# Decode scores of a hybrid decoder step: multiply-and-sum on VectorE, or products on VectorE and sums on ScalarE

## The chip, the cores and the metric

The kernel runs on one core of a Trainium2 chip. The metric is the device time of one execution in microseconds (us). TensorE (PE) multiplies matrices, with PEld its weight loads; VectorE (DVE), ScalarE (ACT) and GpSimd (POOL) work on tiles; SyncE (SP) issues transfers, and so does GpSimd. Each engine takes its instructions in the order in which the program wrote them and waits at each for what it needs.

## The reference

One layer of a decoder: a prompt of 512 rows and 32 sample rows (8 sequences of 4 new tokens), 2048 channels. One input projection feeds four branches of 512 channels (a gated MLP "A", a convolution "B", the forgetting attention "C", FoX, and an attention into 256 memory tokens "M"). Each branch is gated, projected back to 2048 channels, weighted by a sigmoid and added; an output projection and a layer norm follow. All is fp32.

The change is in the attention of the sample rows. In branch C each of the 8 sequences has 1024 cached keys and values, in 8 pages of 128 rows that a page table scatters over a pool; in branch M it has 256 memory keys, 2 pages of 128:

```python
logits = einsum('bqhd,bkhd->bhqk', q, k_all) * HD ** -0.5    # 4 heads of 128 channels, 4 queries
logits = logits + (cq[..., None] - ck[:, :, None, :])        # FoX only
out = einsum('bhqk,bkhd->bqhd', softmax(logits), v_all)
```

So there are (8 x 8 + 8 x 2) = 80 pages, and for each of them 4 queries x 4 heads = 16 columns of scores (128 keys by one), 1280 in all.

## The kernel before, in words

**Pieces.** The matrix work is a list of 677 pieces, one after the other. A piece loads a weight block of 128 x 512 numbers (L257, SP), splits it into a high and a low part (L237 a Copy on ScalarE, L238 a subtraction on VectorE, tile `whl`, four buffers, three pieces ahead; loads run four further) and does 24 matmuls of 272 columns (L268, `mm_k`). By number: 0 to 15 are the projection Q_C, 16 the forget gate, 17 to 32 K_C, 33 to 48 V_C, 49 to 64 Q_M, 65 to 96 the memory projections (every second of these carries side work), 97 to 112 V_A, 113 to 128 U_A, 129 to 144 G_A, 145 to 224 the gates of branch A (`add_gates`: eight times eight pieces with sigmoids at the end, then two with a product), 225 to 240 G_M, 241 to 320 the gates of M, 321 to 336 A_B, 337 to 352 B_B, 353 to 368 G_C, 369 to 448 the gates of C, and so on. Eight pieces share one accumulation, two pieces in the branch projections; then it is evacuated from four PSUM banks: the first half of the columns right behind the last piece's matmuls (`std_mm`, `evac_col`), the second half at the start of the next.

**Side work.** Everything else is written as Python generators, whose `yield`s are the places where the program goes on with the matmuls. In `std_mm`, ahead of its own matmuls, each piece runs a few steps of two chains (`side.step`; a `yield 1` ends the chain's turn for this piece, so such a generator gets one step a piece), then some steps of the score generator (`side.vector(rate(p.i))`). The order of the instructions in every engine's queue is the order in which this program ran.

**Scores.** `v_scores` is started by the second step of `t_qtok("qc")`, so that piece 19 is the first with `side.vector`. It goes through the 80 pages: three sequences of C, all eight of M, the other five of C. A page of keys is gathered into one of the two buffers of `kr` (by GpSimd from the page table, L775, or by SP for the memory, L584), the four queries of a sequence are spread over the partitions into `qb` (one buffer, SP, L590). For each of 16 (query, head), L604 multiplies 128 columns of `kr` and `qb` and adds them up into one column of the score tile `L` (`Lm` for M), then yields.

**Decode.** After the last page of C, `t_decode("qc")` is added to chain 0: forget biases (`t_bias`, 5 steps), transposes, softmax and the transposed weights (steps 6 to 12), then 16 rounds (two groups of four sequences, eight pages each), two steps a round; a round is eight records of matmuls (L756) with four gathered pages of values, `vr`, and the loads run two rounds ahead (`load_v(i + nv)`). `final` then writes the result over the queries. It is wanted in `ev_gate` of G_C, first called behind the matmuls of piece 360; what is not done then is run to its end at once, without matmuls in between:

```python
if br not in B:
    side.finish(*[tasks[t] for t in wait])      # ("ac", "dqc") for brC
```

For branch M the same holds behind piece 232 (`dqm`).

**Slots.** Large tiles share 18 slots; one that is given a slot waits until its last user is done. Eight hold the input rows (`xh`, `xl`) throughout. `qb` holds one while the scores run.

Of the kernel before, what the change touches and what calls it, by code (L numbers as in the profile page):

```python
# [10 lines left out]
AF = mybir.ActivationFunctionType  # L11
ALU = mybir.AluOpType
# [7 lines left out]
NPG = 8  # L20
# [69 lines left out]
def hybrid_step(ctx: ExitStack, tc: tile.TileContext, I, O):  # L90
    nc = tc.nc
    V, S, G, T, SP = nc.vector, nc.scalar, nc.gpsimd, nc.tensor, nc.sync
# [9 lines left out]
    def nm(p):  # L102
        cnt[0] += 1
        return f"{p}{cnt[0]}"

    def slot(shape, dt=F32, n="slot"):
        return big.tile(shape, dt, tag="slot", bufs=18, name=nm(n))

    def kt_t(shape, dt=F32, n="kt"):
        return big.tile(shape, dt, tag="kt", bufs=3, name=nm(n))  # L110

    def s2(shape, dt=F32, n="s2"):
        return big.tile(shape, dt, tag="s2", bufs=5, name=nm(n))
# [10 lines left out]
    def ct(shape, dt=F32, n="c"):  # L124
        return const.tile(shape, dt, name=nm(n))
# [13 lines left out]
    side = Side()  # L139
# [132 lines left out]
    def std_mm(p):  # L272
        mv = p.mov()
        n = p.steps
        if marks["dw"] <= p.i < marks["pw"] and pieces[p.i - 1].last:
            n = (n[0], 0)
        side.step(n)
        side.vector(rate(p.i))
        for c in range(2):
            for k in range(2):  # L280
                mm_k(p, mv, c, k)
            side.flush()
        if p.last:
            p.later = evac_col(p, 0)
# [50 lines left out]
    tasks = {}  # L335
# [218 lines left out]
    S_ = {}  # L554

    def t_qtok(k):
        sm = sample(B[k])
        yield
        b = ps()
        tok_major(B[k], 4, b, sm)  # L560
        yield
        t = s2([32, 512], n="qt")
        V.tensor_copy(out=t, in_=b[0:32])
        SP.dma_start(out=qscr[k], in_=t)
        if k == "qc":
            side.vec = v_scores()
        yield

    def v_scores():
        batches = [("qc", b, NPG) for b in range(3)] + [("qm", b, 2) for b in range(8)] + \  # L570
                  [("qc", b, NPG) for b in range(3, 8)]
        S_["qc"] = kt_t([128, 1056], n="L")
        kr = kt_t([128, 2, 512], n="kr")
        qb = slot([128, 4, 512], n="qb")
        pages = [(k, b, pg, i) for i, (k, b, n) in enumerate(batches) for pg in range(n)]
        done = {"qc": 0, "qm": 0}

        def load_page(n):
            if n < len(pages):
                k, b, pg, _ = pages[n]  # L580
                if k == "qc":
                    gpage(kr[:, n % 2], ck, b, pg)
                else:
                    SP.dma_start(out=kr[:, n % 2], in_=cmk[b, pg * 128:(pg + 1) * 128].rearrange("p h d -> p (h d)"))  # L584

        def load_q(i, t):
            if i < len(batches):
                k, b, _ = batches[i]
                r = b * 4 + t
                SP.dma_start(out=qb[:, t], in_=qscr[k][r:r + 1].rearrange("o c -> (o c)").partition_broadcast(128))  # L590

        load_page(0)
        for t in range(4):
            load_q(0, t)
        for _ in range(24):
            yield
        for n, (k, b, pg, i) in enumerate(pages):
            if k == "qm" and k not in S_:
                S_[k] = s2([128, 256], n="Lm")
            for t in range(4):  # L600
                for h in range(4):
                    o = pg * 128 + h * 32 + b * 4 + t
                    junk = S_["junk"] if "junk" in S_ else S_.setdefault("junk", ct([128, 128], n="junk"))
                    V.tensor_tensor_reduce(out=junk, in0=kr[:, n % 2, h * 128:(h + 1) * 128],  # L604
                                           in1=qb[:, t, h * 128:(h + 1) * 128], op0=ALU.mult, op1=ALU.add, scale=1.0,
                                           scalar=0.0, accum_out=S_[k][:, o:o + 1])
                    yield
                if t == 0:
                    load_page(n + 1)
                if t == 0 and pg == 0 and i:  # L610
                    load_q(i, 3)
                if t and pg == batches[i][2] - 1:
                    load_q(i + 1, t - 1)
            if pg == batches[i][2] - 1:
                done[k] += 1
                if done[k] == 8:
                    tasks["d" + k] = side.add(t_decode(k), 0)

    def t_new():

# [152 lines left out]
    def gpage(dst, src, b, pg):  # L773
        j = b * NPG + pg
        G.indirect_dma_start(out=dst, out_offset=None, in_=src,  # L775
                             in_offset=bass.IndirectOffsetOnAxis(ap=idx[:, j:j + 1], axis=0))
# [31 lines left out]
    def m_mm(p):  # L808
        side.step(p.steps if p.wi == 0 else (0, 0))
        side.vector(rate(p.i) if p.wi == 0 else 0)  # L810
        m = mem["T"][:, p.kt // 2 % 2]
        if p.kt == 0:
            for j in range(2):
                mem["a", p.wi, j] = accb()
        for j in range(2):
            for mp, wp in ((0, 0), (0, 1), (1, 0)):
                T.matmul(out=mem["a", p.wi, j], lhsT=m[:, mp, (2 * (p.kt % 2) + j) * 128:(2 * (p.kt % 2) + j + 1) * 128],  # L817
                         rhs=p.w[:, wp], start=p.kt == 0 and mp == 0 and wp == 0, stop=p.kt == 15 and mp == 1)
        side.flush()
# [515 lines left out]
    marks = {}  # L1335
# [27 lines left out]
            pieces.append(p)  # L1363

    def rate(i):
        return 4 if i < marks["gates"] else 5

    at = {
        marks["conv"]: lambda: side.add(t_cconv(), 1),
# [11 lines left out]
    with tc.manual_schedule():  # L1381
        n = len(pieces)
# [113 lines left out]
```

## Time and profile before

Three runs: 1960.68, 1962.4 and 1965.9 us, median 1962.4.

| | |
|---|---|
| the profiled execution's own time | 1961.29 us |
| its span | 1959.6 us |
| TensorE busy, share, matmuls | 1930.0 us, 98%, 14687 |
| weight loads | 1859.4 us, 95% |
| VectorE | 1221.3 us, 62% |
| ScalarE | 621.2 us, 32% |
| GpSimd | 233.4 us, 12% |

Busy time is the union of the instructions on an engine. TensorE's matmuls are pipelined, so its busy share is not its share of the peak. The score loop's first instruction starts at 108.1 us, its last at 1010.5 us.

### The profile page before, as it was taken

To read this page: it belongs to the slowest core of one execution; us is meant where nothing else is said; L and a number is where in the kernel's file an instruction comes from. 1 tells how busy PE (TensorE), PEld (TensorE's weight loads), DVE (VectorE), ACT (ScalarE), POOL (GpSimd) and SP (SyncE) were. 2 spreads that over 40 slices of the span, in tenths; PEclk is the share of its full clock that TensorE was granted. 3 is DMA by queue.
4 is the path that set the end of the run, shared out by engine and by line. 5 is a ranking of instruction groups with operands and counts; after the bars stand their busy time and mean duration, and the time that the engine had idled before them with its cause. 6 is when DMAs were issued, how large, how long until landed. Compare 5 with 4: busy or idle time off the path is not lost.

```text
span 1959.6 us, 38230 instructions
## 1 busy us (share of the span) xinstructions
PE 1930.0 (98%) x14687; PEld 1859.4 (95%) x14687; DVE 1221.3 (62%) x4107; ACT 621.2 (32%) x1164; POOL 233.4 (12%) x265
## 2 busy tenths in 40 slices
PE   8999999999999999999999999999999999999997
PEld 7999989999999899999999889999999999999985
DVE  4265797877777778877763238767645323256687
ACT  3222353444223222222222223222243222244442
POOL 0000100010000001121225430110110101010000
PEclk9999999999999999999999999999999999999999
DMA  5444465324555544444437663333323333346664
GB/s 167 112 121 113 141 194 153 94 80 135 165 175 176 168 138 121 132 135 117 137 97 209 191 181 87 87 90 89 87 76 90 89 87 88 90 138 219 202 213 161
DMA packets 211601, 261.85 MB, mean 134 GB/s; under 512 B 18251, under 2 KB 171355, under 8 KB 210617
## 3 DMA queue, kind: packets, MB, share of 16 engines
q1 hardware_dynamic: 200297, 224.55, 40.0%
q0 software_dynamic: 10544, 33.80, 5.6%
q8 instruction: 115, 1.88, 0.4%
q10 hardware_dynamic: 576, 1.05, 0.1%
q14 instruction: 69, 0.57, 0.1%
HBM read 250.85 MB, written 8.49 MB: 132 GB/s over the span
## 4 chain that ended last, share of the span: by engine, by line
PE 81%; DVE 3%; DMA 2%; issue 1%; ACT 1%; SPq 0%; POOL 0%; DVEq 0%; ACTq 0%; POOLq 0%
PE acc L268 72%; PE acc L1272 3%; PE acc L817 2%; DMA raw<-in_w_out_dram 1%; PE ps L756 1%; DVE whl L238 1%; DMA qb<-qqm 0%; DVE junk L604 0%; DMA vr<-in_cache_mem_v_dram 0%; PE ps L849 0%; PE ps L870 0%; PE ps L507 0%; PE ps L533 0%; DVE cvt L1082 0%; PE ps L1212 0%
## 5 line engine op out<-in xcount | busy, mean ns | idle before, releaser
L268 PE MATMUL acc<-xh,whl 128*128 128x272 f32 x7168 | 1233.9, 290 | 4.1 <-DVE sg L901 2.5
L268 PEld LDWEIGHTS acc<-xh,whl 128*128 128x128 f32 x7168 | 1021.4, 189 | 23.0 <-ACT whl L237 7.5
L237 ACT ACTIVATE whl<-raw 128x512 fp32r<-128x512 f32 x664 | 418.3, 632 | 1129.1 <-PE acc L268 974.5
L238 DVE TENSOR_TENSOR whl<-raw,whl 128x512 fp32r<-128x512 f32 x664 | 464.4, 703 | 461.7 <-ACT whl L237 459.0
L268 PE MATMUL acc<-xl,whl 128*128 128x272 f32 x3584 | 740.1, 288 | 0.0
L268 PEld LDWEIGHTS acc<-xl,whl 128*128 128x128 f32 x3584 | 564.1, 189 | 0.0
L604 DVE CUSTOM_DVE_ANT_0 junk<-kr,qb 128x128 f32<-128x128 f32 x1280 | 379.4, 296 | 49.8 <-DMA qb<-qqm 8.9
L268 PE MATMUL acc<-bh,whl 128*128 128x272 f32 x1024 | 176.1, 289 | 1.3 <-ACT gs L918 1.3
L930 POOL TENSOR_TENSOR h<-h,gs 128x272 f32<-128x272 f32 x96 | 79.1, 851 | 608.1 <-DVE gs L929 608.0
L268 PEld LDWEIGHTS acc<-bh,whl 128*128 128x128 f32 x1024 | 146.2, 188 | 2.0 <-ACT gs L918 1.5
L775 POOL DMA_INDIRECT kr<-in_cache_k_dram,idx x64 | 65.7, 1027 | 683.4 <-DVE L L604 496.9
L268 PE MATMUL acc<-hh,whl 128*128 128x288 f32 x512 | 107.0, 298 | 0.0
L268 PE MATMUL acc<-bl,whl 128*128 128x272 f32 x512 | 105.6, 288 | 0.0
L1098 DVE SCALAR_TENSOR_TENSOR yb<-hb,wdwc,yb 128x512 f32<-128x512 f32 x120 | 93.4, 778 | 2.1
L604 DVE DVE_READ_ACCUMULATOR2_ANT L<- 128x1 f32 x1024 | 83.5, 82 | 0.0
L268 PEld LDWEIGHTS acc<-hh,whl 128*128 128x128 f32 x512 | 83.4, 188 | 0.1
L268 PEld LDWEIGHTS acc<-bl,whl 128*128 128x128 f32 x512 | 80.5, 189 | 0.0
L268 PE MATMUL acc<-hl,whl 128*128 128x288 f32 x256 | 75.5, 295 | 0.0
L775 POOL DMA_INDIRECT vr<-in_cache_v_dram,idx x64 | 65.5, 1023 | 57.1 <-PE ps L756 40.5
L1272 PE MATMUL acc<-whl,hh 128*128 128x512 f32 x216 | 68.0, 395 | 0.3 <-DVE whl L238 0.2
L918 ACT ACTIVATE gs<-acc 128x272 f32<-128x272 f32 x128 | 43.8, 395 | 47.0 <-PE acc L268 46.3
L1272 PEld LDWEIGHTS acc<-whl,hh 128*128 128x128 f32 x216 | 40.4, 188 | 10.0 <-DVE whl L238 0.8
(326 smaller groups left out, 1093.8 us busy)
## 6 DMA issues: line engine op xcount, KB each, us to landing
raw<-in_w_in_dram SPq DMA_DIRECT2D x446, 256.0 KB, 2.8
raw<-in_w_out_dram SPq DMA_DIRECT2D x128, 256.0 KB, 3.5
raw<-in_w_branch_dram SPq DMA_DIRECT2D x64, 256.0 KB, 2.7
qb<-qqc SPq DMA_DIRECT2D x32, 256.0 KB, 4.3
qb<-qqm SPq DMA_DIRECT2D x32, 256.0 KB, 4.0
raw<-in_w_mem_k_dram SPq DMA_DIRECT2D x16, 256.0 KB, 2.7
raw<-in_w_mem_v_dram SPq DMA_DIRECT2D x16, 256.0 KB, 3.6
kr<-in_cache_mem_k_dram SPq DMA_DIRECT2D x16, 256.0 KB, 3.2
```

Source lines behind the costliest of these rows:

```text
L237: S.activation(out=hi, in_=src, func=AF.Copy)
L238: side.later(lambda: V.tensor_tensor(out=lo, in0=src, in1=hi.bitcast(F32), op=ALU.subtract))
L268: T.matmul(out=p.st[c][i][:, 0:hi - lo], lhsT=p.w[:, wp, k, c * 128:(c + 1) * 128], rhs=mv[mp][:, p.k0 + k, lo:hi], start=p.first and k == ...
L604: V.tensor_tensor_reduce(out=junk, in0=kr[:, n % 2, h * 128:(h + 1) * 128], in1=qb[:, t, h * 128:(h + 1) * 128], op0=ALU.mult, op1=ALU.add ...
L756: T.matmul(out=ob[32 * j:32 * j + 32, :], lhsT=PT[:, pg, 4 * g + j, :], rhs=vr[:, j, :], start=pg == 0, stop=pg == npg - 1 and not fox)
L775: G.indirect_dma_start(out=dst, out_offset=None, in_=src, in_offset=bass.IndirectOffsetOnAxis(ap=idx[:, j:j + 1], axis=0))
L817: T.matmul(out=mem["a", p.wi, j], lhsT=m[:, mp, (2 * (p.kt % 2) + j) * 128:(2 * (p.kt % 2) + j + 1) * 128], rhs=p.w[:, wp], start=p.kt == ...
L918: S.activation(out=sgs[0][:, c, hf, :], in_=a, func=AF.Sigmoid)
L930: G.tensor_tensor(out=hd, in0=hd, in1=s, op=ALU.add)
L1098: V.scalar_tensor_tensor(out=yv, in0=hv, scalar=wdw[:, j, c:c + 1], in1=yv, op0=ALU.mult, op1=ALU.add)
L1272: T.matmul(out=oacc[p.nb, j], lhsT=hhl[p.kt // 4][mp][:, p.kt % 4, o:o + 128], rhs=p.w[:, wp], start=p.kt == 0 and mp == 0 and wp == 0, st ...
```

## The change

The score loop works on half a page of queries at a time. One VectorE product forms the 1024 columns of two queries (the page's keys are read twice, by a repeated operand) in one of the two halves of a new tile `prod`, which holds a slot while the scores run; eight ScalarE Copies with an accumulated output then sum 128 columns each. The sums of one half come behind the product of the next (`behind`). Every product and every sum is a step. The loads of the next sequence's queries are issued two and two behind the products of the last page, and the score generator runs five steps a piece throughout.

```diff
@@ -594,27 +594,38 @@
+        prod = slot([128, 2, 2, 512], n="prod")
+        junk = ct([128, 128], n="junk")
+
+        def sums(k, b, pg, half):
+
+            for t in range(2):
+                for h in range(4):
+                    o = pg * 128 + h * 32 + b * 4 + 2 * half + t
+                    S.activation(out=junk, in_=prod[:, half, t, h * 128:(h + 1) * 128], func=AF.Copy,
+                                 accum_out=S_[k][:, o:o + 1])
+                    yield
+            if half and pg == dict(qc=NPG, qm=2)[k] - 1:
+                done[k] += 1
+                if done[k] == 8:
+                    tasks["d" + k] = side.add(t_decode(k), 0)
+
+        behind = iter(())
         for n, (k, b, pg, i) in enumerate(pages):
             if k == "qm" and k not in S_:
                 S_[k] = s2([128, 256], n="Lm")
-            for t in range(4):
-                for h in range(4):
-                    o = pg * 128 + h * 32 + b * 4 + t
-                    junk = S_["junk"] if "junk" in S_ else S_.setdefault("junk", ct([128, 128], n="junk"))
-                    V.tensor_tensor_reduce(out=junk, in0=kr[:, n % 2, h * 128:(h + 1) * 128],
-                                           in1=qb[:, t, h * 128:(h + 1) * 128], op0=ALU.mult, op1=ALU.add, scale=1.0,
-                                           scalar=0.0, accum_out=S_[k][:, o:o + 1])
-                    yield
-                if t == 0:
+            for half in range(2):
+                V.tensor_tensor(out=prod[:, half], in0=kr[:, n % 2].unsqueeze(1).to_broadcast([128, 2, 512]),
+                                in1=qb[:, 2 * half:2 * half + 2], op=ALU.mult)
+                yield
+                if half == 0:
                     load_page(n + 1)
-                if t == 0 and pg == 0 and i:
-                    load_q(i, 3)
-                if t and pg == batches[i][2] - 1:
-                    load_q(i + 1, t - 1)
-            if pg == batches[i][2] - 1:
-                done[k] += 1
-                if done[k] == 8:
-                    tasks["d" + k] = side.add(t_decode(k), 0)
+                if pg == batches[i][2] - 1:
+                    for t in range(2):
+                        load_q(i + 1, 2 * half + t)
+                yield from behind
+                behind = sums(k, b, pg, half)
+        yield from behind
 
@@ -1363,7 +1374,7 @@
     def rate(i):
-        return 4 if i < marks["gates"] else 5
+        return 5
```

## Rows read from the trace of the kernel before

**Rows 1.** The page's span and busy times: engine, busy us, share, instructions.
```profile
span 1959.6 us, 38230 instructions
...
PE 1930.0 (98%) x14687; PEld 1859.4 (95%) x14687; DVE 1221.3 (62%) x4107; ACT 621.2 (32%) x1164; POOL 233.4 (12%) x265
```

**Rows 2.** Waits of TensorE: waiter, releaser, us in total, times, longest.
```profile
PE ps L993 <- DVE cA L989: 3.0, 1, 3.0
...
PE acc L268 <- DVE h L927: 1.1, 1, 1.1
...
PE acc L268 <- ACT ua L941: 0.5, 1, 0.5
```

**Rows 3.** Windows: stretch, us, busy time (instructions) of PE, PEld, DVE, ACT, POOL, clock, DMA.
```profile
625.00:1012.00 387.00, 385.72 (x3073) 381.45 (x3072) 296.17 (x1468) 103.04 (x192) 60.45 (x70) 1.00 0.47 135
```

**Rows 4.** Windows, around the wait of L993; the granted clock is third from last.
```profile
378.00:381.20 3.20, 0.24 (x2) 0.02 (x1) 3.15 (x8) 0.63 (x1) 0.00 (x0) 0.96 0.30 79
381.20:384.40 3.20, 3.17 (x15) 3.14 (x16) 2.99 (x20) 0.00 (x0) 0.00 (x0) 0.50 0.14 20
```

**Rows 5.** Groups by line and form, L604: busy us, mean ns, idle before, releasers.
```profile
L604 DVE CUSTOM_DVE_ANT_0 junk<-kr,qb 128x128 f32<-128x128 f32 x1280 | 379.4, 296 | 49.8 <-DMA qb<-qqm 8.9 <-DMA qb<-qqc 5.6 <-DVE Lm L604 0.8
...
L604 DVE DVE_READ_ACCUMULATOR2_ANT L<- 128x1 f32 x1024 | 83.5, 82 | 0.0
...
L604 DVE DVE_READ_ACCUMULATOR2_ANT Lm<- 128x1 f32 x256 | 20.9, 82 | 0.0
```

**Rows 6.** Groups by line and form, nearest operations: products, copies, Exp, a table load.
```profile
L237 ACT ACTIVATE whl<-raw 128x512 fp32r<-128x512 f32 x664 | 418.3, 632 | 1129.1 <-PE acc L268 974.5 <-issue 68.3 <-PE acc L1272 20.2
...
L1082 DVE TENSOR_TENSOR cvt<-hs,wdwc 128x992 f32<-128x992 f32 x4 | 8.0, 1991 | 0.0
...
L234 DVE TENSOR_TENSOR hl<-h,hh 128x1024 fp32r<-128x1024 f32 x4 | 4.9, 1218 | 0.0
...
L766 DVE COPY Oall<-ps 128x512 f32<-128x512 f32 x4 | 2.8, 690 | 10.4 <-PE ps L760 7.8 <-PE ps L756 2.7
...
L485 ACT ACTIVATE P<-P,nmx 128x512 f32<-128x512 f32 x4 | 2.9, 724 | 6.2 <-DVE nmx L483 6.2
...
L485 ACT ACTIVATE P<-P,nmx 128x128 f32<-128x128 f32 x4 | 1.6, 402 | 1.5 <-DVE nmx L483 1.5
...
L941 ACT ACT_TABLE_LOAD x2 | 2.6, 1283 | 0.0
```

**Rows 7.** Timeline of ACT, an Exp with accumulated output: start, us, instruction.
```profile
388.39 0.51 ACT L485 ACTIVATE P<-P,nmx 128x256 f32<-128x256 f32 x1 [0.38 <-DVE nmx L483]
388.81 0.19 ACT L485 ACTIVATION_READ_ACCUMULATOR P<-P,nmx 128x1 f32 x1
388.90 0.50 ACT L485 ACTIVATE P<-P,nmx 128x256 f32<-128x256 f32 x1
```

**Rows 8.** Timeline of PE around the end of piece 360.
```profile
1165.74 1.06 PE L756 MATMUL ps<-vr,PTs 128*32 128x512 f32 x8
1166.74 1.06 PE L760 MATMUL ps<-rows,PnT 32*32 32x512 f32 x8
...
1170.83 0.60 PE L746 MATMUL ps<-ident,Oall 128*128 128x128 f32 x4
1172.82 0.74 PE L268 MATMUL acc<-xh,whl 128*128 128x272 f32 x2 [1.39 <-DVE sg L901]
```

**Rows 9.** The chain that ended last, 1054 to 1062 us: start, us, what.
```profile
1054.37 1.00 PE ps L756 x8
...
1061.57 1.00 PE ps L756 x8
```

**Rows 10.** Timeline of POOL: the first two gathers behind round 0.
```profile
1055.74 0.95 POOL L775 DMA_INDIRECT vr<-in_cache_v_dram,idx  x1 [10.30 <-PE ps L756]
1056.99 0.95 POOL L775 DMA_INDIRECT vr<-in_cache_v_dram,idx  x1 [0.30 <-issue]
```

**Rows 11.** One line, L775 (all gathers): from issue to landing.
```profile
DMA to landing us min/median/max: 3.2/3.8/5.8
```

## The prediction

> **What bounds the kernel now.** I read the page's busy times first [rows 1]: TensorE is busy for 1930 of the span's 1959.6 us. Then its waits [rows 2]: of what is left, the score stage (108 to 1011 us) has three that the change can touch, 3.0 us for L989's copy, 1.1 us for L927, 0.5 us for a GELU (L941). Then the stretches [rows 3]: where the score loop runs longest undisturbed, 625 to 1012 us, TensorE is busy 385.7 of 387 us beside a VectorE at 77% and a ScalarE at 27%. So TensorE sets the pace, and taking work off VectorE is worth only what those waits cost. One of them costs twice: after the 3 us of idleness before L993 the granted clock is 0.50 (the lower level, 1.2 GHz) from 381.2 to 384.4 us [rows 4], so that one piece of 3.0 us took about 1.5 us more. The most to be won is 3.0 + 1.5 + 1.1 = 5.6 us.
>
> **What the scores cost now and will cost.** L604's 1280 instructions are 379.4 us and the reads of the accumulator 83.5 and 20.9 [rows 5]: 484 us of VectorE. The new product has 1024 columns, two SBUF operands, fp32; nearest is L234's 128x1024, 1.22 us, and the far bound L1082's product with a strided broadcast operand, 1.99 us for 992 columns [rows 6]. Here the broadcast operand repeats a whole row of 512, columns adjacent, so I take 1.22: 160 x 1.22 = 195 us, 289 us less for VectorE (165 us less at 1.99).
>
> ScalarE gets 1280 ACTIVATEs of 128 columns, each with a read of its accumulator. The trace has the pair only as Exp over 256 columns: 0.51 us from one start to the next, the read adding 0.09 of it beyond the ACTIVATE's end [rows 7]. A Copy of 512 columns from SBUF takes 632 ns, and Exp 402 ns for 128 columns and 724 for 512, so 0.84 ns a column [rows 6]: a Copy of 128 is some 632 - 384 x 0.84 = 309 ns, less 0.09 of overlap with what follows, plus 0.09 for the read, 0.31 us a sum. Bounds: 0.22 (the read free) to 0.50 (309 + 190 ns, nothing overlapped). I take 0.31, nearest to rows 7: 1280 x 0.31 = 397 us on top of ScalarE's 621 [rows 1]. Five steps a piece, 40 sums in 45 of them, are 4.44 x 0.31 = 1.4 us; with the weight split (about 0.54 of its 0.63 us not overlapped) 1.9 us of a piece's 3.0. L237 waited 974 us for TensorE in all [rows 6], so ScalarE has the room on average.
>
> Per score the two engines together will be busy about 0.46 us (0.31 + 195/1280), against 0.38 (484/1280) before. The Trainium skill, "ScalarE: Activation LUTs", Rules for kernel authors, speaks against such a move: additions and multiplications belong on VectorE, not ScalarE; it calls VectorE up to about three times faster per element in bf16. By that rule, which the two figures bear out in sign (in fp32 and by less), the work is dearer where it goes, and ScalarE could become the bound: the first rival below.
>
> **What is lost on ScalarE.** Its queue is in order, and a piece's sums stand ahead of its own evacuation. In plain pieces an evacuation after 0.54 + 5 x 0.31 us is ready at 2.8 us, before TensorE wants the bank at 3.0. Where a table load of 1.28 us stands ahead of it as well (six evacuations: L941, L938 and L900, two each, one of these rows in [rows 6]) the cover is thinner: L941 already made TensorE wait 0.5 [rows 2], so 1.5 us more are bare there; a second such place gives perhaps 1.0, a third 0.4; the others have room. 2.9 us; bounds 0 and 6 x 1.55 = 9.3. The product waits for the last sum of two halves before, which is issued just ahead of it; that holds up VectorE's weight subtraction, queued behind, by up to 2 us, but it is wanted only three pieces (9 us) later. The query loads move up: all four are issued 17 steps (some 10 us) ahead of their use, and the waits for them in front of the score instructions [rows 5], behind which L927's 1.1 us came about, should go. On SP's queue they hold up weight loads by at most one product; these run four pieces ahead.
>
> **When the scores end.** Count the calls of the score generator from piece 19 on. Before: pieces 19 to 64, 16 memory pieces, pieces 97 to 144, 110 in all at 4 calls = 440, then 5 a piece. It ends in call 24 + 1280 + 1 = 1305, and (1305 - 440)/5 = 173 pieces after 144: piece 317. After: 550 calls by piece 144, and 24 + 160 + 1280 + 1 = 1465 in all, since each product is a step too: (1465 - 550)/5 = 183, piece 327. The memory scores end at piece 184 instead of 189; both are far ahead of 232, where they are wanted. The FoX decode starts one piece later, one step a piece: round i of its 16 weighted sums (L756) is its step 13 + 2i. Before, round 15 fell on piece 360 exactly, the piece whose evacuation wants the decode finished (`side.finish` in `ev_gate`, brC). The trace shows this [rows 8]: round 15 and L760, one piece of matmuls, the last transposes, then the first gate with a wait of 1.39 us. **After, piece 360 carries round 10, and rounds 11 to 15 run in one burst behind it.**
>
> **What the burst costs.** Spaced two pieces apart (7.2 us) [rows 9] the rounds hid their gathers; in the burst nothing does. A round needs four gathers, 1.25 us apart on GpSimd [rows 10], the last landing 3.8 us after its issue [rows 11]: 7.6 us from the first. A gather into a slot starts about 0.4 us after the round that frees it (round 0 ends at 1055.4, the next gather starts at 1055.74). At piece 360 fifteen of 18 slots hold other tiles, the convolution's `yb` takes one more there, two are left for pages. With t = 0 at round 10: it ends at 1.0, piece 360 at 4.1, round 11 at 5.1, round 12 at 6.1 (both loaded). Round 13's gathers start when 11 has freed its slot, 5.5, ready 13.1. Round 14's: GpSimd is free at 10.5, ready 18.1. Round 15's: slot free at 14.5, GpSimd at 15.5, ready 23.1. Then 1.0 + 1.0 (L760), a copy of 512 columns 0.7 (L766, [rows 6]), transposes 0.6, copy and gate 0.9 (less than the 1.39 of [rows 8], which held other work too): the next piece at 27.3. TensorE's own work in this is 1 + 3 + 5 + 1 + 0.6 = 10.6, idle 16.7; before 1.39. That is +15.3. By [rows 4] an idle time of 3 us puts the clock to 0.50: the end of the burst (2.6 us of matmuls) at half clock costs +2.5. Together +17.8. Bounds: with a third slot free, round 13's gathers start at round 10's end, which saves 4 us, and with the clock kept up 2.5 more: +11; with every landing at the longest of [rows 11], 5.8, and half clock into the next piece: +22.
>
> **Sum.** -5.6 + 2.9 + 17.8 = +15.1 us on the profiled execution's 1961.3 us (1.1 us below the median of 1962.4): 1976.4 us.
>
> **Rivals.** (1) ScalarE becomes the bound. With 0.50 us a sum, the last piece of a sigmoid pair puts 0.54 + 2.5 + 0.7 (two sigmoids of 272 columns, by the same slope) = 3.7 us ahead of TensorE's next bank at 3.0; 18 such pairs (eight in each of two gate stages, two of G_M) x 0.7 = 13 us: 1989. For it: Exp's read lasts 0.19 us. Against it: only 0.09 of that is left bare [rows 7].
> (2) The other side: the burst is covered and the kernel is faster. GpSimd's queue does not follow the pieces, only its slots; with four or more slots free for pages at piece 360 the gathers of rounds 13 to 15 would be under way before TensorE comes to them, and the finish would cost no more than the 1.4 us of before. Then 1961.3 - 5.6 + 0 to 2.9 = 1956 to 1959. Against it: the gather of [rows 10] sat idle for 10.3 us until round 0 freed its slot.
> (3) Half a burst: the scores run out earlier than counted or TensorE finds more pages there, and one or two rounds are bare: some 7 us, 1966. For it: the count rests on every yield.
>
> **Chances.** Forecast 0.66 (own range 1967 to 1986; 0.04 of it within 0.3%). Rival 1 0.10, slower. Rival 2 0.16, half of it faster by over 0.3% (5.9 us, about what a measurement of this kernel tells from no change), half within. Rival 3 0.08, within. Slower 0.62 + 0.10 = 0.72, within 0.04 + 0.08 + 0.08 = 0.20, faster 0.08. The range, 1962 to 1990, leaves out rival 2 and the ends of the forecast's own spread.
>
> **What would show it.** Right: after the scores, in front of brC's first gate, L756 with waits for `vr` gathers of 4 to 7 us and granted clock 0.50 there; sums on ScalarE 0.3 us apart; no wait before L993; VectorE some 290 us less busy. Wrong: L756 at that place without waits (rival 2), or TensorE waiting for ScalarE's evacuations all through the gate stages (rival 1); the prediction fails if the finish in front of brC costs under 10 us.

## The result and the profile after

The changed kernel takes 2013.22 us (median of 4 runs, 2011.22 to 2015.14), the kernel before 1962.72 beside it: a ratio of 1.0258 [1.0246, 1.0271]. That is 50 us more, where 15 were forecast and 28 were the upper end of the range. The sign was right, the size was not.

The page of the changed kernel, span and busy time of each engine (as [rows 1]):

```profile
span 2009.6 us, 38549 instructions
...
PE 1952.5 (97%) x14687; PEld 1865.9 (93%) x14687; DVE 1046.1 (52%) x1707; ACT 1093.1 (54%) x3724; POOL 248.3 (12%) x265
```

TensorE has its 14687 matmuls as before, and yet 22 us more of busy time. That isn't more work. Some 3.4 us of it are two more stretches at half clock (an estimate: in each, 3.4 us of busy time do the work of 1.7; they are shown below). Of the rest, much is waiting that is shown as work: matmuls' ends are modelled, and where a group of them trickles, waiting for its operands, part of the wait counts as busy. The Trainium skill, "Perfetto Trace Analysis", Tensor Engine Instruction, says that TensorE's end times are computed from the instruction's size, not observed. The trace agrees: the burst below is some 8 us of work and shows 15.76 us of busy time. So the lost time is better read from the start of the same piece in both traces than from waits. Each piece has a fixed number of matmuls, so counting them finds the piece. Time gained (-) or lost by each kernel against the one before, in us, worked out in this way from one profiled execution of each (the columns behind the changed kernel's are experiments of the next section):

```
                               before's   changed  two    sums   both   changed  two tiles+last
pieces (stage)                 length              tiles  last          at 317   at 317
0-64   (f, K_C, V_C, Q_M)       232.9      +3.7    +2.1   +2.3   +0.7    +2.4     +3.3
65-96  (memory K, V)             56.4      +7.7    +1.8   +7.0   +1.4    +2.5      0.0
97-144 (V_A, U_A, G_A)          186.6     +12.9    +7.8   +8.5   +4.2    +8.0     -0.9
145-224 (gates A)               249.9      +5.4    +1.5   +1.2   -2.1    +9.7     -1.7
225-320 (G_M, gates M)          289.8      +8.8    +4.9   +5.7   +0.7   +13.3     +1.2
sum up to piece 320                       +38.5   +18.1  +24.7   +4.9   +35.9     +1.9
321-352 (A_B, B_B)              115.2      -6.4    -6.1   -6.3   -6.5    -0.1     -0.1
353-360 and the finish           33.8     +18.2   +22.4  +22.0  +18.1     0.0      0.0
```

The figures are good to some 0.2 us, and two executions differ by more: pieces 0 to 16, ahead of the first score step, took 73.4 to 75.8 us in the profiles, and 1.8 of the last column's +3.3 lie there.

Two losses, then: 38.5 us spread over the whole score loop, and a burst of 18.2 us at one place, of which 6.4 us are matmuls that were moved there, so 11.8 net. Behind piece 360 the changed kernel keeps within 0.1 us of the one before, up to the output stage, which is 0.9 us shorter.

**The score loop.** The groups of the sums and the product (as [rows 5]; busy us, mean ns, idle before, releasers), then five instructions of ScalarE's timeline in the changed kernel (as [rows 7]; start, us, instruction):

```profile
L605 ACT ACTIVATE junk<-prod 128x128 f32<-128x128 f32 x1280 | 393.7, 308 | 31.2
L605 ACT ACTIVATION_READ_ACCUMULATOR junk<-prod 128x1 f32 x1280 | 239.6, 187 | 0.0
L618 DVE TENSOR_TENSOR prod<-kr,qb 128x1024 f32<-128x1024 f32 x160 | 197.0, 1231 | 332.8 <-ACT junk L605 328.2 <-DMA raw<-in_w_in_dram 2.3 <-DMA raw<-in_w_branch_dram 2.2
```

```profile
562.12 0.31 ACT L605 ACTIVATE junk<-prod 128x128 f32<-128x128 f32 x1
562.33 0.19 ACT L605 ACTIVATION_READ_ACCUMULATOR junk<-prod 128x1 f32 x1
562.55 0.31 ACT L605 ACTIVATE junk<-prod 128x128 f32<-128x128 f32 x1
562.77 0.18 ACT L605 ACTIVATION_READ_ACCUMULATOR junk<-prod 128x1 f32 x1
562.99 0.31 ACT L605 ACTIVATE junk<-prod 128x128 f32<-128x128 f32 x1
```

The durations are as forecast: 308 ns for the ACTIVATE (309 worked out), 187 for the read, 1231 for the product (1220 taken). But the sums start 0.43 us apart (562.12, 562.55, 562.99), not 0.31: the next one begins 0.03 us after the read has ended, where the Exp pair of [rows 7] began 0.09 after the read's start. Five sums are 2.2 us of ScalarE, not 1.5.

What that does is seen at one place, the first gate of branch A. ScalarE, TensorE and the granted clock (third from last in the window) there, in the changed kernel:

```profile
472.12 0.29 ACT L605 ACTIVATE junk<-prod 128x128 f32<-128x128 f32 x1
...
473.84 0.31 ACT L605 ACTIVATE junk<-prod 128x128 f32<-128x128 f32 x1
474.05 0.19 ACT L605 ACTIVATION_READ_ACCUMULATOR junk<-prod 128x1 f32 x1
474.26 1.28 ACT L911 ACT_TABLE_LOAD   x1
475.55 1.27 ACT L911 ACTIVATE sg<-acc 128x272 f32<-128x272 f32 x4
```

```profile
474.17 0.60 PE L871 MATMUL ps<-ident,P 128*128 128x128 f32 x4
476.48 0.74 PE L268 MATMUL acc<-xh,whl 128*128 128x272 f32 x2 [1.71 <-DVE sg L912]
```

```profile
477.60:481.00 3.40, 3.40 (x18) 3.40 (x17) 1.91 (x6) 1.29 (x3) 0.00 (x0) 0.50 0.00 0
```

Five sums stand ahead of the table load; the sigmoid begins at 475.55, VectorE's product with it (L912) follows, and TensorE, finished with the transposes by 474.8, waits 1.71 us for the bank. Behind that wait the granted clock is 0.50 for 3.4 us, as in [rows 4]. So the wait costs twice: piece 136, in which it falls, takes 5.5 us from start to start (3.6 before), and piece 137, behind it, 5.5 (3.8 before). The changed kernel has three such stretches in the score stage (from 306.9, 399.1 and 477.6), the one before had one. The largest waits of TensorE (as [rows 2]):

```profile
PE acc L268 <- DVE sg L912: 6.7, 6, 1.7
...
PE acc L268 <- DVE gs L940: 3.5, 4, 1.5
PE ps L1004 <- DVE cA L1000: 3.5, 1, 3.5
PE acc L828 <- DVE whl L238: 3.2, 3, 2.0
```

Two of these are VectorE at second hand: `sg` and `gs` wait for ScalarE's sigmoids. The weight subtraction L238 is queued behind a product, and the products wait 328 us in all for sums. And L1000 is the copy of [rows 2] (L989 before), whose wait was to go: it is 3.5 us.

ScalarE had the least room in the memory stage: only every second piece carries score steps there, but every piece brings a weight split, so that two splits go with a turn of five steps. Busy times in the memory stage, first of the kernel before, then of the changed one (ACT is the fourth):

```profile
241.20:297.50 56.30, 56.30 (x294) 47.25 (x293) 50.60 (x196) 29.06 (x56) 5.58 (x5) 1.00 0.63 197
```

```profile
245.30:309.30 64.00, 59.25 (x294) 47.92 (x293) 44.40 (x79) 52.88 (x196) 5.57 (x5) 0.98 0.61 190
```

ScalarE goes from 52% to 83% of the stage (52.88 of 64.00), and the stage takes 7.7 us more.

**The burst.** TensorE and GpSimd in front of the next piece, in the changed kernel (as [rows 8, 10]):

```profile
1204.93 2.76 PE L767 MATMUL ps<-vr,PTs 128*32 128x512 f32 x18
1208.78 5.54 PE L767 MATMUL ps<-vr,PTs 128*32 128x512 f32 x12 [1.09 <-DMA vr<-in_cache_v_dram,idx]
1214.77 1.05 PE L767 MATMUL ps<-vr,PTs 128*32 128x512 f32 x2 [0.45 <-DMA vr<-in_cache_v_dram,idx]
1216.30 2.95 PE L767 MATMUL ps<-vr,PTs 128*32 128x512 f32 x6 [0.48 <-DMA vr<-in_cache_v_dram,idx]
1219.54 1.04 PE L767 MATMUL ps<-vr,PTs 128*32 128x512 f32 x2 [0.28 <-DMA vr<-in_cache_v_dram,idx]
1220.51 1.06 PE L771 MATMUL ps<-rows,PnT 32*32 32x512 f32 x8
1222.38 0.66 PE L757 MATMUL ps<-ident,Oall 128*128 128x128 f32 x4 [0.81 <-DVE Oall L777]
1223.70 0.74 PE L268 MATMUL acc<-xh,whl 128*128 128x272 f32 x2 [0.66 <-DVE sg L912]
```

```profile
1202.18 1.10 POOL L786 DMA_INDIRECT vr<-in_cache_v_dram,idx  x1 [4.34 <-PE ps L767]
1203.59 0.95 POOL L786 DMA_INDIRECT vr<-in_cache_v_dram,idx  x1 [0.30 <-issue]
...
1216.09 0.94 POOL L786 DMA_INDIRECT vr<-in_cache_v_dram,idx  x1 [0.30 <-issue]
```

```profile
1203.90:1223.70 19.80, 15.76 (x61) 3.60 (x60) 1.31 (x4) 0.89 (x3) 10.08 (x11) 1.00 0.58 171
```

Forty matmuls, 18 + 12 + 2 + 6 + 2, eight a round: rounds 11 to 15 in one burst behind piece 360, as forecast. The last three rounds' twelve gathers run back to back on GpSimd from the end of round 10, 1.25 us apart, and TensorE follows them gather by gather. No wait exceeds 1.1 us and PE looks 80% busy (15.76 of 19.80), though the same forty matmuls take 5 us when their pages are loaded (8 in 1.06 us, [rows 8]). That is why the waits for `vr` of 4 to 7 us, which were to show the burst, aren't seen: most of the waiting stands between matmuls that the profile calls busy.

### The profile page after: what moved, and what is told of

It is laid out like the page before. It is cut to its first block, busy times and chain, and to the rows that moved or that the text cites. A ratio compares the mean times of both kernels' runs of the same rounds, so it can differ in the third digit from the quotient of the medians.

```text
span 2009.6 us, 38549 instructions
## 1 busy us (share of the span) xinstructions
PE 1952.5 (97%) x14687; PEld 1865.9 (93%) x14687; DVE 1046.1 (52%) x1707; ACT 1093.1 (54%) x3724; POOL 248.3 (12%) x265
## 4 chain that ended last, share of the span: by engine, by line
PE 82%; ACT 8%; DVE 4%; issue 3%; DMA 2%; POOL 1%; SPq 0%; ACTq 0%; DVEq 0%; POOLq 0%
PE acc L268 74%; ACT junk L605 4%; PE acc L1283 3%; ACT whl L237 2%; POOL vr L786 1%; DVE whl L238 1%; DMA raw<-in_w_out_dram 1%; PE ps L767 1%; PE ps L248 0%; ACT P L485 0%; PE acc L404 0%; DMA vr<-in_cache_mem_v_dram 0%; PE ps L507 0%; DVE nmx L483 0%; DVE cvt L1093 0%
## 5 line engine op out<-in xcount | busy, mean ns | idle before, releaser
L238 DVE TENSOR_TENSOR whl<-raw,whl 128x512 fp32r<-128x512 f32 x664 | 465.3, 707 | 401.5 <-ACT whl L237 399.6
L605 ACT ACTIVATE junk<-prod 128x128 f32<-128x128 f32 x1280 | 393.7, 308 | 31.2
L618 DVE TENSOR_TENSOR prod<-kr,qb 128x1024 f32<-128x1024 f32 x160 | 197.0, 1231 | 332.8 <-ACT junk L605 328.2
L605 ACT ACTIVATION_READ_ACCUMULATOR junk<-prod 128x1 f32 x1280 | 239.6, 187 | 0.0
L786 POOL DMA_INDIRECT kr<-in_cache_k_dram,idx x64 | 74.8, 1169 | 679.1 <-DVE prod L618 666.7
L941 POOL TENSOR_TENSOR h<-h,gs 128x272 f32<-128x272 f32 x96 | 83.5, 898 | 594.4 <-DVE gs L940 594.4
```

What stands on the lines that cost most here:

```text
L238: side.later(lambda: V.tensor_tensor(out=lo, in0=src, in1=hi.bitcast(F32), op=ALU.subtract))
L605: S.activation(out=junk, in_=prod[:, half, t, h * 128:(h + 1) * 128], func=AF.Copy, accum_out=S_[k][:, o:o + 1])
L618: V.tensor_tensor(out=prod[:, half], in0=kr[:, n % 2].unsqueeze(1).to_broadcast([128, 2, 512]), in1=qb[:, 2 * half:2 * half + 2], op=ALU.mult)
L786: G.indirect_dma_start(out=dst, out_offset=None, in_=src, in_offset=bass.IndirectOffsetOnAxis(ap=idx[:, j:j + 1], axis=0))
L941: G.tensor_tensor(out=hd, in0=hd, in1=s, op=ALU.add)
```

## The experiments

**Is it ScalarE's sums at all, or the steps, the product and the loads?** The sums of a half as one VectorE instruction, in the first of their eight steps; everything else as changed:

```
-                    S.activation(out=junk, in_=prod[:, half, t, h * 128:(h + 1) * 128], func=AF.Copy,
-                                 accum_out=S_[k][:, o:o + 1])
+                    if t == 0 and h == 0:
+                        V.tensor_reduce(out=S_[k][:, pg * 128:(pg + 1) * 128].rearrange("p (h y) -> p h y", h=4)
+                                        [:, :, b * 4 + 2 * half:b * 4 + 2 * half + 2],
+                                        in_=prod[:, half].rearrange("p t (h c) -> p h t c", h=4), axis=AX.X, op=ALU.add)
```

> The changed kernel with the eight sums on ScalarE replaced by one reduction of the 1024 products on VectorE; steps, loads, the product tile and the end of the scores at piece 327 stay. Theory (the loss up to piece 320 is ScalarE's work and nothing else of the change): the 38 us go and the burst stays: 1963 + 12 = 1975, less up to 5 us for the waits of before that VectorE's relief takes away (484 us of score work become some 390). Rival (the pace of five steps, the moved query loads or the held slot cost the 38 us): over 1995.

Measured: 1983.62 us, ratio 1.0093 [1.0076, 1.0110]. Up to piece 320 the stages together differ from before by 0.0 us, and the burst is there (+20.9 us at its place). So the 38.5 us are the sums on ScalarE alone; the steps, the product and the query loads cost nothing there. The time is above the 1975 expected for another reason, which the next run has as well.

**The end of the scores alone.** The kernel before, its FoX decode started 50 steps (ten pieces) later:

```
   done[k] += 1
+  if done[k] == 8 and k == "qc":
+      for _ in range(50):
+          yield
   if done[k] == 8:
       (t_decode is added)
```

> The kernel before, with the FoX decode handed over 50 steps (ten pieces) after the last score, so at piece 327 as in the changed kernel; nothing else. Theory of the burst: rounds 11 to 15 run behind piece 360 and the stretch from piece 353 to 361 grows by about 18 us, while the 16 us before it get some 6 us shorter because these rounds no longer stand there: 1962.7 + 12 = 1975. Rival (the burst costs only because ScalarE was late as well): no more than 1966.

Measured: 1981.12 us, ratio 1.0073 [1.0051, 1.0095]; +20.2 us at the place of the burst, -0.7 in pieces 321 to 352, 0.0 up to piece 320. The burst needs nothing of the change but the later end: piece 360 with the finish takes 22.3 us, 22.0 in the changed kernel and 5.1 before. But 1975 was expected, with pieces 321 to 352 some 6 us shorter, as in the changed kernel. They aren't, since pieces 327 to 329 take 15.0 us here (9.0 in the changed kernel), and piece 354 is 1.7 us longer as well. In the reduce version these two are 6.4 and 2.2 us. ScalarE's weight splits wait there for something that the trace doesn't name (5.86 us there and 7.44 at piece 354, marked `remote`), while gathers land (the DMA engines are 86% busy from 1044 to 1047.4 us). What starts it was not tested; it is no part of the burst. Behind the burst the granted clock does fall here:

```profile
1193.40:1196.80 3.40, 3.40 (x16) 3.40 (x17) 2.35 (x7) 0.86 (x2) 0.00 (x0) 0.50 0.01 2
```

**Why 0.43 us a sum?** All sums write one tile, `junk`. In the instruction stream each ACTIVATE of L605 waits for a semaphore of ScalarE itself, which the read of the sum before counts up; the second Exp of [rows 7] waits for none. Two tiles in turn, both in bf16:

```
-  junk = ct([128, 128], n="junk")
+  junk = [ct([128, 128], mybir.dt.bfloat16, n="junk") for _ in range(2)]
-  S.activation(out=junk, ...)
+  S.activation(out=junk[h % 2], ...)
```

> The changed kernel, with the sums' unwanted products written to two bf16 tiles in turn instead of always the same fp32 one (the accumulated sums are as before). In the changed kernel the sums start 0.435 us apart, because each waits for the one before it to have written the same tile; the prediction had 0.31. Theory A (this wait on itself is what made ScalarE too slow): sums 0.31 us apart, ScalarE some 150 us less occupied, the 38 us lost up to piece 320 shrink to under 12: about 1980 to 1988. Theory B (it is the order in ScalarE's queue, sums ahead of weight splits and evacuations, whatever a sum costs): over 2000. If the sums stay 0.43 apart, the wait is on the column of scores and not on this tile, and nothing changes: 2013.

Measured: 1995.5 us, ratio 1.0152 [1.0135, 1.0168]. The spacing came out as expected:

```profile
561.06 0.29 ACT L605 ACTIVATE junk<-prod 128x128 bf16<-128x128 f32 x1
561.26 0.19 ACT L605 ACTIVATION_READ_ACCUMULATOR junk<-prod 128x1 f32 x1
561.35 0.30 ACT L605 ACTIVATE junk<-prod 128x128 bf16<-128x128 f32 x1
...
561.65 0.30 ACT L605 ACTIVATE junk<-prod 128x128 bf16<-128x128 f32 x1
```

0.29 to 0.30 us: the next sum starts 0.10 us before the read has ended. It still has a wait for that semaphore, but the sum that last wrote its tile is now the one before the last. The time did not come out as expected (1980 to 1988), as 18.1 us of loss stay up to piece 320. As that edit also narrows the output, a control has one tile, in bf16:

```
-  junk = ct([128, 128], n="junk")
+  junk = ct([128, 128], mybir.dt.bfloat16, n="junk")
```

> The changed kernel with one junk tile as before, but in bf16: what the version with two tiles changed beside their number. Theory (a sum waits for the sum before it because both write the same tile): the sums stay 0.43 us apart and the time within 2 us of the changed kernel, 2010 to 2016 us. Rival (the narrower output is what shortened them): 0.30 us apart, 1993 to 1998 us.

Measured: 2014.11 us, ratio 1.0273 [1.0256, 1.0290], the loss up to piece 320 at 37.3 us:

```profile
564.47 0.31 ACT L605 ACTIVATE junk<-prod 128x128 bf16<-128x128 f32 x1
564.68 0.19 ACT L605 ACTIVATION_READ_ACCUMULATOR junk<-prod 128x1 f32 x1
564.90 0.31 ACT L605 ACTIVATE junk<-prod 128x128 bf16<-128x128 f32 x1
```

The width of the tile makes no difference; it is the shared tile: 38.5 - 18.1 = 20.4 us.

**The place in the queue.** The changed kernel with a piece's score steps issued behind its matmuls and the first half of its evacuations:

```
   side.step(n)
-  side.vector(rate(p.i))
   (the piece's matmuls)
   if p.last:
       p.later = evac_col(p, 0)
+  side.vector(rate(p.i))
```

> The changed kernel with the score steps of the plain pieces moved behind the matmuls and the first half of the evacuation (side.vector after evac_col in std_mm), so that the sums no longer stand ahead of the evacuation of their own piece. Theory B (order in the queue): TensorE's waits for evacuations (L912, L940, L952, L938) go and the gate and projection stages lose 15 to 25 us less: about 1990; the memory stage, whose loop is another, keeps its 8 us. Theory A (a sum is too dear, ScalarE is full): no more than 8 us better, over 2005.

Measured: 1999.59 us, ratio 1.0169 [1.0152, 1.0186]. That is more than the 1990 expected, but the loss up to piece 320 falls by 13.8 us to 24.7, and the products' wait for sums from 328 to 69 us. The memory stage, whose loop the edit doesn't touch, keeps its +7.0. Both edits together:

> The changed kernel with both edits on ScalarE: the sums write two tiles in turn, and they are issued behind the piece's matmuls and its first evacuations. Theory (two causes that add up: the wait of each sum for the one before, and the sums' place ahead of the evacuations in an in-order queue): by piece 320 one edit alone took the loss from 38 to 18 us, the other from 38 to 24; both together leave 4 to 8 us there, the burst of weighted sums stays: 1980 to 1986 us. Rival A (what is left after the first edit is the amount of work on ScalarE, 1280 sums of 0.30 us, wherever they stand): the loss to piece 320 stays near 18 us, 1993 to 1997 us.

Measured: 1979.61 us, ratio 1.0077 [1.0060, 1.0094], the loss up to piece 320 4.9 us. The two causes add up (20.4 + 13.8 = 34.2, together 33.6), and of the loss at most the 4.9 us that are left can be the mere amount of work on ScalarE: the 1280 sums are all still there.

**Repairing the end.** The product takes no step of its own and the pace is that of before, so that the scores end at piece 317:

```
   V.tensor_tensor(out=prod[:, half], ...)
-  yield
...
   def rate(i):
-      return 5
+      return 4 if i < marks["gates"] else 5
```

The changed kernel with this alone:

> The changed kernel in the steps and pace of before: the product takes no step of its own, the pace is 4 and then 5, the scores end at piece 317. The sums stay on ScalarE, into one tile, ahead of the matmuls. Theory: the burst goes (12 to 16 us net), the sums' loss up to piece 320 stays at 34 to 40 us: 1997 to 2003 us. Rival (the fifth step a piece before the gate stages is what loads ScalarE in the memory stage and the three stages behind it): the loss to piece 320 falls to 22 to 28 us as well: 1984 to 1991 us.

Measured: 1998.54 us, ratio 1.0183 [1.0166, 1.0200]: the burst is gone to the last 0.1 us, and the sums' loss stays at 35.9. By the medians the kernel is 14.7 us shorter; by the stages 11.8 of that is the burst and 2.6 the smaller loss. Its rival was right in part: at four steps a piece the memory stage loses 2.5 us instead of 7.7. The gate stages lose more, 9.7 + 13.3. The reduce with this, and all three repairs:

> The scores as VectorE products of 1024 columns, each followed by one VectorE tensor_reduce over the channels, in the steps and pace of the kernel before: the product takes no step of its own and the pace is 4 and then 5, so that the scores end at piece 317 as before. Theory (the burst comes from the scores' end ten pieces later, nothing else): no burst in front of the convolution's first gate, 1960 to 1967 us, no different from before, with some 90 us less VectorE work. Rival (the product's form or its slot of a tile brings the burst): 1979 to 1984 us, as the reduce in 1465 steps had it.

> All three repairs: two tiles in turn, the sums behind the piece's matmuls, the scores' end at piece 317. Theory: 1964 to 1971 us, about as long as before or up to 0.4% longer, the waits of before in the score stage included. Rival A (amount of ScalarE work): 1978 to 1983 us.

Measured: 1961.97 us, ratio 0.9989 [0.9979, 0.9999], and 1961.64 us, ratio 0.9991 [0.9982, 1.0001]. Both losses are gone, and each kernel is level with the one before: at most 0.2% faster, by intervals that end at no difference. The last was better than expected. ScalarE at the gate shown above, in the kernel with all three:

```profile
454.57 1.28 ACT L910 ACT_TABLE_LOAD   x1
455.87 0.69 ACT L910 ACTIVATE sg<-acc 128x272 f32<-128x272 f32 x2
456.44 0.31 ACT L605 ACTIVATE junk<-prod 128x128 bf16<-128x128 f32 x1
```

Four sums now stand behind the first two sigmoids, and TensorE has no wait there. The wait for the copy L1000 (L999 here) is half of the 3.0 us of before, and this kernel, alone of them all, has no stretch at 0.50 in the score stage:

```profile
PE ps L1003 <- DVE cA L999: 1.5, 1, 1.5
```

Even so its time is that of before: of some 3 us that this should save (1.5 of the wait, 1.5 of the clock, by [rows 4]), pieces 97 to 144 keep 0.9.

In the reduce version my "some 90 us less VectorE work" was wrong. Its page has VectorE at:

```profile
PE 1929.9 (98%) x14687; PEld 1859.5 (95%) x14687; DVE 1221.9 (62%) x1867; ACT 621.0 (32%) x1164; POOL 238.7 (12%) x265
```

1221.9 us, as before [rows 1]; the next section says why.

**The wait that didn't go.** The copy ahead of the small matmul L993 (L1004 in the changed kernel), with two more steps between them, in the reduce version and in the kernel before:

```
   V.tensor_copy(out=wsT, in_=b)
   yield
   yield
+  yield
+  yield
```

> The reduce version with the scores' end at piece 317, and the copy of the transposed mixing weights two more steps ahead of the matmul that reads it, so that TensorE comes to that matmul one piece or so later. Theory (the 3.3 us wait that the change left standing is the copy's place behind VectorE's normalisation and weight split, and costs its 3.3 us and about 1.5 us of half clock behind it): 1956 to 1959 us, 0.25 to 0.4% faster than before. Rival (the wait only moves to the next matmul that needs the normalised rows): 1960 to 1963 us.

> The kernel before with the same two steps between the copy and the matmul. Theory: the wait of 3.0 us and 1.5 us of half clock go here as well, 1957 to 1960 us: the wait was one of place, not of VectorE's load by the scores. Rival: it stays or moves, 1961 to 1964 us.

Measured: 1965.96 us, ratio 0.9990 [0.9981, 0.9999], and 1965.32 us, ratio 0.9989 [0.9980, 0.9998]. The theory fell: the kernel before was 1967.31 us in that round, so that 1.4 and 2.0 us are won, not 4.5 or more. The wait for the copy is gone from both, but one of about the same size has come up a little later; the first of the two kernels:

```profile
PE acc L268 <- ACT ua L952: 2.8, 1, 2.8
```

With a half clock behind it (from 393.0 us) it costs most of what was won. The two traces also show 3.0 and 4.6 us more than before in the pieces 353 to 360. That isn't the decode, whose rounds fall on the same pieces as before: it is piece 354 alone, where a weight split waits as in the kernel with the later decode. In the second of the two kernels:

```profile
1150.58 0.63 ACT L237 ACTIVATE whl<-raw 128x512 fp32r<-128x512 f32 x1 [7.68 <-remote]
```

Whether the edit has a part in that was not tested. Removing the wait for the copy alone wins 0.2% at most.

## Why the prediction was wrong

**The step that failed: the price of a sum, and what is lost on ScalarE by it.** "ScalarE gets 1280 ACTIVATEs ... 0.31 us a sum", and from it "2.9 us; bounds 0 and 9.3". Both durations were right and the overlap was not. It came from a pair in which each instruction writes other columns; the sums all write one tile, and each waits for the one before: 0.43 us. It lies within the bounds (0.22 to 0.50), but the term built on it does not hold even with 0.30: two tiles still lose 18.1 us. The second fault is in the term itself. It counted six evacuations with a table load and took the others to have room by a piece of 3.0 us, with ScalarE's average for a witness. It left out the memory stage, with two weight splits where a plain piece has one (52% to 83% busy, +7.7 us), and most of the sigmoids that feed VectorE and through it TensorE: `sg` only where a table load stands ahead, `gs` not at all. And it let the products' wait for sums cost nothing, at "up to 2 us" with nine to spare; the waits are 2.05 us on average (328 in all), but in the memory stage the weight subtraction behind them made TensorE wait 3.2 us. Measured for the term: 38.5 us. With a tile of its own for each second sum and the sums behind the evacuations it is 4.9, near what was forecast.

Rival 1 had the right mechanism, at a smaller price: by its formula 0.54 + 5 x 0.43 + 0.7 = 3.4 us for the last piece of a sigmoid pair, 0.4 over, times 18, 7 us. The gate and G stages from 129 on lost 5.8 + 5.4 + 8.8 = 20.0. It left out the table load and the way through VectorE. Its sign, TensorE waiting for ScalarE's evacuations all through the gate stages, came true in part; of the forecast's own signs none did as stated: sums 0.43 us apart instead of 0.3, VectorE 175 us less busy instead of 290, a wait ahead of the small matmul, and in the burst no long waits and no half clock.

**The waits of before: -5.6, measured about none of it.** The prediction gave no reason why the copy's wait should go but the average relief. L927's 1.1 us became 1.7 in three waits (L938 in the changed kernel), L941's 0.5 became 2.5 (L952), and L993's 3.0 stayed, at 3.5. VectorE had no more time in front of that copy than before, in the changed kernel:

```profile
393.87 1.22 DVE L618 TENSOR_TENSOR prod<-kr,qb 128x1024 f32<-128x1024 f32 x1
395.01 0.69 DVE L238 TENSOR_TENSOR whl<-raw,whl 128x512 fp32r<-128x512 f32 x1
395.61 0.75 DVE L992 SCALAR_TENSOR_TENSOR vta<-vta,cA 128x512 f32<-128x512 f32 x1
...
397.26 0.68 DVE L1000 COPY cA<-ps 128x512 f32<-128x512 f32 x1
```

One whole product of 1.22 us stands where four multiply-and-sums of 0.33 stood. The relief is an average over pieces; in this one the engine was as full as ever. With the scores' end at 317 the relief does show: the wait is 1.6 and 1.5 us with the sums on ScalarE, and 3.3 with the reduce.

**VectorE's relief: 289 us forecast, 175 measured** (1221.3 to 1046.1). The prediction added the reads of the accumulator to the instructions, 379.4 + 104.4. But a read lies inside the time of its instruction, but for some 0.01 us; the kernel before:

```profile
372.30 0.28 DVE L604 CUSTOM_DVE_ANT_0 junk<-kr,qb 128x128 f32<-128x128 f32 x1
372.51 0.08 DVE L604 DVE_READ_ACCUMULATOR2_ANT L<- 128x1 f32 x1
372.63 0.29 DVE L604 CUSTOM_DVE_ANT_0 junk<-kr,qb 128x128 f32<-128x128 f32 x1
```

So the reads added almost nothing to the engine's busy time: the instructions' 379.4 us less 197.0 for the products are 182, near the 175 measured. That is also why product and reduce together cost VectorE what the old form did.

**The end of the scores and the burst: right in mechanism, -6 us in size.** Piece 327, rounds 11 to 15 behind piece 360, gathers as the limit, no sign of rival 2: all as forecast, and the burst goes when the count of steps does. +17.8 was taken, 11.8 net measured (18.2 - 6.4). A third slot was free, so that the gathers ran on from round 10's end, and the clock stayed at 1.00; this is the forecast's lower bound, +11. In five of the six other kernels with the burst a stretch at 0.50 follows it, but it costs little: piece 360 takes 21.9 to 22.3 us in all seven, and pieces 361 to 368 are at most 0.3 us longer than before. What four of the kernels show at this place beyond 18 us lies at pieces 353 and 354, ahead of the burst. So the +2.5 for the clock had nothing to show for it in any of them.

Sum: 38.5 + 11.8 = 50.3. With +0.5 ahead of the first piece and -0.9 in the output stage that is the 50.0 between the two spans (2009.6 and 1959.6).

**On the rule weighed in the prediction**, that sums belong on VectorE (the Trainium skill, "ScalarE: Activation LUTs", Rules for kernel authors), the trace agrees, and by more than was granted there, as far as the price goes. In the reduce version eight sums are one VectorE instruction of 1.21 us:

```profile
L605 DVE TENSOR_REDUCE L<-prod 128x8 f32<-128x1024 f32 x128 | 154.9, 1210 | 0.0
```

On ScalarE they are 8 x 0.43 = 3.5 us, or 2.4 us at their best. The time follows the rule only in part: TensorE sets the pace, and with order, tiles and pace mended the kernel with the sums on ScalarE is as fast as the one with the reduce (1961.64 and 1961.97 us).

## What to carry to other kernels

When work moves to an engine with room, ask what each instruction waits for on that engine itself: a scratch output that nobody reads still orders its writers, and two scratch tiles in turn removed that here. Then ask what stands behind the new work in that engine's queue, in the stage where it has the least room, not on average; work that nobody waits for belongs behind the evacuations. And in code that advances by steps, a new `yield` is a schedule: here 160 of them, 32 pieces' worth, of which the quicker pace took back only 22, put five rounds of gathers in front of TensorE.

## What the runs showed of the hardware

On ScalarE a sum that waits for the sum just before it starts 0.14 us later (0.43 against 0.29 us a sum): only after the accumulator's read has ended, instead of beside it. The wait as such isn't the price: with two tiles in turn each sum still waits for ScalarE's own semaphore, for an earlier sum, and they start 0.29 to 0.30 us apart. For VectorE the Trainium skill, "VectorE: DVE Perf Modes", The DRAIN you can't avoid, measured that semaphores between successive copies cost nothing extra; no run here tests that engine, and on ScalarE, with accumulator reads, it does not carry over.

A wait of 1.7 us behind which the granted clock is 0.50 for 3.4 us (477.6 to 481.0) costs twice: some 2 us in its own piece and 1.8 in the next, against the kernel before. A burst in which matmuls trickle with the landing gathers kept 1.00 all through (1203.9 to 1223.7), though TensorE had some 8 us of work in 20 (five rounds 5.0, L771 1.0, the transposes 0.6, the end of piece 360 1.0). The same burst had 0.50 behind it in the kernel before with the later decode and in four others; what tells them apart was not tested.
